# Turning 32x32 blocks by row copies in a hybrid RWKV-7 / HGRN2 layer

## The chip, the cores and the metric

The kernel runs on one core of one Trainium2 chip. The metric is the device time of one execution in microseconds (us). The core's engines are TensorE (PE in the profile, PEld for its weight loads), VectorE (DVE), ScalarE (ACT), GpSimd (POOL) and SyncE (SP); SP issues nearly all DMAs.

## The reference

One layer over x of shape (1, 512, 2048) in float32, with D_RWKV = D_HGRN = 1024, 16 RWKV heads of 64 and 8 HGRN heads of 128:

```python
proj = jnp.einsum('btd,dc->btc', h, w_in[l])              # 2048 -> 4224 + 4096 columns
rw = _token_shift(proj[..., :RWKV_COLS], shift_mu[l])
hg = proj[..., RWKV_COLS:]
o_rwkv, _ = _rwkv7_branch(rw, ...)
o_hgrn = _hgrn2_branch(hg, ...)
y = jnp.einsum('btc,cd->btd', jnp.concatenate([o_rwkv, o_hgrn], -1), w_out[l])
h = _layer_norm(ALPHA * h + y, ln_w[l], ln_b[l])

# RWKV, per frame t and head (S is 64 x 64)
sa = S @ a_t
S = S * w_t + sa b_t^T + v_t k_t^T
o_t = S @ r_t
# then group norm over the head, * gn_w + gn_b, + sum(r k r_k) * v, * silu(z)

# HGRN, per chunk of frames and head (S is 128 x 128), b = cumsum(log f)
att = (q_t exp(b_t - b_s)) . k_s  for s <= t
o = att @ i + (q exp(b)) @ S
S = S * exp(b_last) + (k exp(b_last - b))^T @ i
# then o * rsqrt(mean(o^2)) * g_norm_w * silu(z)
```

## The kernel before

All float32 products of the two projections are made of three matmuls in a split format (high by high, low by high, high by low). `split` (L405) makes the two halves: ScalarE rounds a block of weights to `wh`, VectorE subtracts to `wl`. Weights come in 156 loads of 512 KB (`load`, L420) into two buffers `wr`; each load holds two parts, and each part feeds 12 main matmuls of 128x512 (`three`, L441). `wh` and `wl` have three buffers each. The input projection runs unit by unit of 128 output columns (`proj`, L472) in the order of `_order` (L39): per group of two RWKV pairs k, r, v, the z of two pairs earlier, and q, f, i, g of two HGRN heads. The output projection (`rows`, L488, and the code below it) follows, and a layer norm.

Everything else is written as generators that yield operations: `rwkv_prep` (a pair of heads: decays, keys, scores), `rwkv_invert`, `rwkv_scan` (eight chunks of 64 frames, two pairs at once), `rwkv_finish` (group norm and gate), `hgrn_heads` and `hgrn_out`. The class `Plan` (L63) interleaves them while the program is built: it keeps a clock for each engine with costs, and after each main matmul it lets the queues of generators issue what could start now (`pump`, `step`). A TensorE operation is issued when its inputs have been ready for 0.35 us (`LEAD`); small TensorE work is grouped into visits (`worth`, `HOLD`). The resulting order on each engine is fixed in the program; at run time the engines go through it in order and wait for semaphores. So the place of an instruction rests on what `Plan` holds to be ready, and a wait that lasts longer on the chip holds up everything behind it on that engine.

Frames must stand on the partitions for some operands and channels for others. There are two ways to turn a block. One is TensorE: `tr` (L320) transposes 128x128 with the identity into PSUM. Before, these turned the keys of a head (`hgrn_out`, three tiles, L1056), the end of a head (four tiles, L1090) and the end of an RWKV pair (`rwkv_finish`, four tiles, L912): 8 x 3 + 8 x 4 + 8 x 4 = 88. The other is `turned` (L385): VectorE transposes each 32x32 block in place (`dtr`), and 16 (or 8) DMAs from SBUF to SBUF, one for each source and target band of 32 partitions, put the blocks where they belong. Before, it turned the keys `bk` and the values `zz` of a pair. Its DMAs stand on SP's queue between the weight loads.

Of the kernel before, what the change touches and what calls it, by code (L numbers as in the profile page):

```python
# [11 lines left out]
ALU = mybir.AluOpType  # L12
# [50 lines left out]
class Plan:  # L63
# [7 lines left out]
    HOLD = {"whole": 0.6, "narrow": 1.0}  # L71
    TURNS = {("main", "whole"): 0.015, ("whole", "main"): 0.033, ("main", "narrow"): 0.1,
             ("whole", "narrow"): 0.1, ("narrow", "main"): 0.26, ("narrow", "whole"): 0.2}
    LEAD = -0.35
    SLACK = 0.6
    EARLY = 0.5

    def __init__(self, room):
        self.clock = {"pe": 0.0, "dve": 0.0, "act": 0.0, "pool": 0.0, "dma": 0.0}
        self.table = None  # L80
        self.mode = "main"
# [153 lines left out]
def mixer_kernel(ctx, tc, head, x_r, w_all, par, up, ln_wb, consts, hmask, out):  # L235
# [122 lines left out]
    def dtr(o, i):  # L358
        return dve_op([i], o, lambda: dve.transpose(o, i), per=0.0019)
# [22 lines left out]
            f = lambda: dve.tensor_copy(o, i)  # L382
        return Op([act_way(o, i, AF.Copy, scale), ("dve", 0.075 + size(o) * 0.00105 + moved(o, i), f)], [i], [o])

    def turned(dst, src, tmp, rows=4, base=0):  # L385


        name = dst.tensor.name
        yield dtr(tmp, src)
        yield lambda: by_now(tmp)  # L390
        for a in range(4):
            for b in range(rows):
                o = base + 32 * b
                nc.sync.dma_start(dst[o : o + 32, :, 32 * a : 32 * a + 32],
                                  tmp[32 * a : 32 * a + 32, :, 32 * b : 32 * b + 32])
# [217 lines left out]
            ups.append(upw)  # L613

    hc = [slice(64 * h, 64 * h + 64) for h in range(2)]

    def rwkv_prep(S, p):
        if p == 0:
# [111 lines left out]
        S["bv"] = r  # L730

        yield room(zz=1)
        z = take("zz", [P, NCH, P])
        yield room(ksq=1)
        tmp = take("ksq")
        yield from turned(z, chunks(v), chunks(tmp), rows=2, base=64)
        drop(v, tmp)
        S["zz"] = z

    def from_v(SS, sc):  # L740

        yield lambda: all("zz" in S for S in SS)
        zs = [S["zz"] for S in SS]
        yield room(main=2, mix=1)
        yield landed(*zs, sc)
        pss = [take("main") for _ in SS]
        for half, (z, ps) in enumerate(zip(zs, pss)):
            for c in range(NCH):
                for h in range(2):
                    yield mm(ps[hc[h], c * C : c * C + C], sc[64:128, 0, half * 16 + 2 * c + h],  # L750
                             z[64:128, c, hc[h]])

        def keep():
            for z, ps in zip(zs, pss):
                for h in range(2):
                    yield copy(z[0:64, :, hc[h]], chunks(ps[hc[h]]))
                drop(ps)

        return keep

    def outputs(SS, sc):

        yield room(mix=2)
        pss = [take("mix") for _ in SS]
        for half, (S, po) in enumerate(zip(SS, pss)):
            z = S["zz"]
            yield lambda z=z: by_now(z)
            for c in range(0, NCH, 2):
                for h in range(2):
                    for e in range(2):  # L770
                        yield mm(po[hc[e], c // 2 * P + 64 * h : c // 2 * P + 64 * h + 64],
                                 sc[:, 1, half * 16 + 2 * (c + e) + h], z[:, c + e, hc[h]])
# [52 lines left out]
    def rwkv_scan(SS, sc):  # L825
# [9 lines left out]
        def block(ps, h):  # L835
            return ps[hc[h], h * 64 : h * 64 + 64]

        for rt, bds, o in zip(rts, bdss, os):
            yield memset(rt[64:128], 0.0)
            for t in bds:  # L840
                yield memset(t, 0.0)
            yield memset(o[0:64, 0], 0.0)
        olds = [None] * 2
        for c in range(NCH):
            more = c < NCH - 1
            zs = [zz[:, c] for zz in zzs]
            news = [bds[c % 2] for bds in bdss]
            pxs = []
            if c > 0:
                yield landed(*olds)  # L850
                yield room(mix=2)
                for ar, old in zip(ars, olds):
                    pxs.append(take("mix"))
                    yield mm(pxs[-1][:, :P], ar[:, c], old)
                for rt, px, z in zip(rts, pxs, zs):
                    yield stt(rt[0:64], px[0:64, :P], -1.0, z[0:64], ALU.mult, ALU.subtract)
                if more:
                    for new, old, pc in zip(news, olds, pcs):
                        yield act(new, old, AF.Copy, scale=pc[:, c : c + 1])
            else:  # L860
                for rt, z in zip(rts, zs):
                    yield copy(rt[0:64], z[0:64], scale=-1.0)
            yield landed(*rts)
            yield room(mix=2)
            psas = [take("mix") for _ in SS]
# [2 lines left out]
                yield mm(psa[:, :P], sc[:, 0, i : i + 2].rearrange("p h t -> p (h t)"), rt)  # L868
            for psa, z in zip(psas, zs):
                for h in range(2):  # L870
                    yield copy(z[0:64, hc[h]], block(psa, h))
# [18 lines left out]
    def rwkv_finish(S, p):  # L890
# [14 lines left out]
        drop(sm, sq)  # L905
# [11 lines left out]
        drop(po)  # L917
        yield stt(z, sz, 1.0, z, ALU.add, ALU.mult)
        yield stt(g, g, hcol(HGB, p), z, ALU.add, ALU.mult)
        drop(z, S["bv"], S["ot"], sz)  # L920
        put_gated(p, g)

    def rwkv_group(SS, grp):
        yield lambda: all("scored" in S for S in SS)
        sc = scores[grp]
        yield from rwkv_invert(SS, sc)

        def run():
            yield from rwkv_scan(SS, sc)
            yield from outputs(SS, sc)  # L930
            drop(sc)
            for i, S in enumerate(SS):
                plan.add(finishes, rwkv_finish(S, 2 * grp + i))

        plan.add(scans[0], run())

# [113 lines left out]
    def hgrn_out(S, h, q, k, dt_, dg, tot, tots):  # L1050
# [1 line left out]
        yield room(g=1)  # L1052
        g = take("g")
        kt, state = tiles(g)[:, 0:3], tiles(k)[:, 0:3]
        yield landed(k)
        ps = take("mix")  # L1056
        for t in range(3):
            yield tr(ps[:, t * P : t * P + P], k[:, t * P : t * P + P])
        yield copy(kt, tiles(ps)[:, 0:3])
        drop(ps)  # L1060
        yield has(S, "i")
        yield room(rs=1)
        i_all = S["i"]
# [25 lines left out]
        yield landed(o2)  # L1089
        pn = take("mix")  # L1090
        for j in range(4):
            yield tr(pn[:, j * P : j * P + P], o2[:, j * P : j * P + P])
        yield has(S, "g")
        yield stt(g, pn, hcol(HHW, h), S["g"], ALU.mult, ALU.mult)
        drop(S["g"], pn, o2)
        put_gated(8 + h, g)

    def silu2(ps, put):
# [24 lines left out]


    scans = [plan.queue(), plan.queue()]
    groups, finishes, preps = plan.queue(), plan.queue(), plan.queue()
    heads, stores = plan.queue(), plan.queue()


# [530 lines left out]
```

## Time and profile before

| what | value |
|---|---|
| three runs | 1053.51, 1053.82, 1051.52 us; median 1053.51 |
| the profiled execution | 1053.89 us |
| its span, first to last instruction | 1052.1 us |
| granted TensorE clock, mean | 0.998 |
| instructions | 18837 |
| DMA packets | 87305, of which 56368 under 512 B |

The profile is of one execution. Its page gives busy time of each engine, the chain of work that ended last, and groups of instructions by source line; a line is often a helper's (L317 is any small matmul, L321 any transposition, L330 a ScalarE copy, L340 a VectorE product or sum, L349 a fused VectorE operation). Names of tiles stand without their numbers. A row of the order of time gives the start, the duration, the engine and line, and what is written from what. Matmuls overlap, so the distance from one start to the next is what an instruction holds of TensorE. A row of a group ends with its busy time, the mean duration in ns of one, and the idle time before it. A row of waits gives the engine and line, what it waited for, the sum in us, the count and the longest.

### The profile page before, as it was taken

To read this page: it belongs to the slowest core of one execution; us is meant where nothing else is said; L and a number is where in the kernel's file an instruction comes from. 1 tells how busy PE (TensorE), PEld (TensorE's weight loads), DVE (VectorE), ACT (ScalarE), POOL (GpSimd) and SP (SyncE) were. 2 spreads that over 40 slices of the span, in tenths; PEclk is the share of its full clock that TensorE was granted. 3 is DMA by queue.
4 is the path that set the end of the run, shared out by engine and by line. 5 is a ranking of instruction groups with operands and counts; after the bars stand their busy time and mean duration, and the time that the engine had idled before them with its cause. 6 is when DMAs were issued, how large, how long until landed. Compare 5 with 4: busy or idle time off the path is not lost.

```text
span 1052.1 us, 18837 instructions
## 1 busy us (share of the span) xinstructions
PE 1042.6 (99%) x7342; PEld 867.6 (82%) x7342; DVE 755.1 (72%) x1653; ACT 438.0 (42%) x867; POOL 37.4 (4%) x81
## 2 busy tenths in 40 slices
PE   9999999999999999999999999999999999999997
PEld 8888888888888888888888888888888788888885
DVE  7475898667769987676688856865998677725556
ACT  6445243444352344552533344525235454323321
POOL 0000000000000000000000000000000001000000
PEclk9999999999999999999999999999999999999999
DMA  8134343222343522223534223234352143545613
GB/s 332 51 104 113 98 112 86 85 79 80 84 123 101 122 80 85 73 91 80 137 83 123 88 66 100 69 91 122 96 125 70 58 166 126 186 128 158 203 61 130
DMA packets 87305, 114.79 MB, mean 109 GB/s; under 512 B 56368, under 2 KB 58160, under 8 KB 87088
## 3 DMA queue, kind: packets, MB, share of 16 engines
q1 hardware_dynamic: 87072, 113.39, 36.5%
q8 instruction: 58, 0.95, 0.4%
q14 instruction: 31, 0.25, 0.1%
q10 hardware_dynamic: 144, 0.20, 0.1%
HBM read 99.92 MB, written 7.34 MB: 102 GB/s over the span
## 4 chain that ended last, share of the span: by engine, by line
PE 99%; DVE 1%; issue 0%; DVEq 0%
PE main L446 74%; PE mix L317 11%; PE mix L446 8%; PE main L1185 3%; PE main L317 2%; PE mix L321 1%; PE mix L1135 0%; DVE inv L349 0%; DVE inv L340 0%; DVE stats L1542 0%; DVEq L1656 0%; DVE mv L1350 0%; DVE mv L345 0%; DVE inv L1133 0%; DVE mv L349 0%
## 5 line engine op out<-in xcount | busy, mean ns | idle before, releaser
L446 PE MATMUL main<-xh,wl 128*128 128x512 f32 x864 | 342.4, 396 | 0.0
L446 PE MATMUL main<-xh,wh 128*128 128x512 f32 x864 | 341.6, 395 | 0.0
L446 PE MATMUL main<-xl,wh 128*128 128x512 f32 x864 | 340.9, 395 | 0.0
L330 ACT ACTIVATE wh<-wr 128x512 fp32r<-128x512 f32 x299 | 186.8, 626 | 234.9 <-PE main L446 167.2
L340 DVE TENSOR_TENSOR wl<-wr,wh 128x512 fp32r<-128x512 f32 x299 | 203.7, 682 | 61.2 <-ACT wh L330 59.7
L446 PEld LDWEIGHTS main<-xh,wl 128*128 128x128 f32 x864 | 162.7, 188 | 33.0
L446 PEld LDWEIGHTS main<-xl,wh 128*128 128x128 f32 x864 | 162.7, 188 | 32.8
L446 PEld LDWEIGHTS main<-xh,wh 128*128 128x128 f32 x864 | 162.8, 188 | 32.6
L446 PE MATMUL main<-wh,xh 128*128 128x512 f32 (+1 forms) x262 | 102.4, 391 | 0.0
L446 PE MATMUL main<-wh,xl 128*128 128x512 f32 (+1 forms) x262 | 102.1, 390 | 0.0
L446 PE MATMUL main<-wl,xh 128*128 128x512 f32 (+1 forms) x262 | 102.1, 390 | 0.0
L446 PEld LDWEIGHTS main<-wl,xh 128*128 128x128 f32 x262 | 49.2, 188 | 9.8
L446 PEld LDWEIGHTS main<-wh,xl 128*128 128x128 f32 x262 | 49.2, 188 | 9.7
L446 PEld LDWEIGHTS main<-wh,xh 128*128 128x128 f32 x262 | 49.2, 188 | 9.5
L331 ACT ACTIVATE t<-main,om 128x512 f32<-128x512 f32 x33 | 22.4, 687 | 53.5 <-PE main L446 42.3
L349 DVE SCALAR_TENSOR_TENSOR t<-main,pr,t 128x511 f32<-128x511 f32 x33 | 24.4, 747 | 28.1 <-ACT t L331 27.7
L340 DVE TENSOR_TENSOR inv<-inv,inv 64x30 f32<-64x30 f32 (+14 forms) x120 | 38.6, 322 | 2.9
L340 DVE TENSOR_TENSOR inv<-inv 64x30 f32<-64x30 f32 (+14 forms) x120 | 38.4, 320 | 2.3
L340 DVE TENSOR_TENSOR t<-t,tot 128x256 f32<-128x256 f32 x96 | 37.9, 415 | 1.9 <-PE mix L317 1.7
L349 DVE SCALAR_TENSOR_TENSOR bd<-mix,pc,bd 64x64 f32<-64x64 f32 x112 | 31.7, 283 | 9.5 <-PE mix L317 7.2
L330 ACT ACTIVATE zz<-mix 64x64 f32<-64x64 f32 x61 | 13.4, 219 | 45.6 <-PE mix L317 43.9
L331 ACT ACTIVATE t<-main 128x512 f32<-128x512 f32 x32 | 18.5, 598 | 30.6 <-PE main L446 30.2
(222 smaller groups left out, 1331.2 us busy)
## 6 DMA issues: line engine op xcount, KB each, us to landing
wr<-w_all SPq DMA_DIRECT2D x156, 512.0 KB, 3.6
q<-head SPq DMA_DIRECT2D x15, 448.0 KB, 5.5
q<-q SPq DMA_DIRECT2D x128, 32.0 KB, 2.4
g<-x_r SPq DMA_DIRECT2D x16, 256.0 KB, 4.0
spill<-g SPq DMA_DIRECT2D x12, 256.0 KB, 2.8
out<-q SPq DMA_DIRECT2D x12, 256.0 KB, 2.4
t<-spill SPq DMA_DIRECT2D x10, 256.0 KB, 4.0
zz<-ksq SPq DMA_DIRECT2D x64, 32.0 KB, 2.7
```

The lines of the kernel that those rows point to most:

```text
L317: return Op([("pe", cost, lambda: pe.matmul(o, l, r, start=start, stop=stop, **kw))], [l, r], [o], mode="narrow" if narrow else "main" if ...
L321: return Op([("pe", 0.11, lambda: pe.transpose(o, i, ident))], [i], [o])
L330: return "act", cost, lambda: sc_e.activation(o, i, f, scale=scale)
L331: return "act", cost, lambda: sc_e.activation(o, i, f, scale=scale, bias=bias)
L340: return dve_op([a, b], o, lambda: dve.tensor_tensor(o, a, b, f), base=0.16 if o.shape[0] < P and size(o) == C and o.tensor.name in tags e ...
L349: return dve_op([a, b], o, lambda: dve.scalar_tensor_tensor(o, a, s, b, f1, f2), per=0.00113, base=0.085 if o.shape[0] == P else 0.25 if s ...
L446: pe.matmul(ps, l, r, start=first and i == 0, stop=last and i == 2)
L1185: pe.matmul(pss[a], *ops, start=k == 0 and low == of == 0, stop=k == KT - 1 and low == 1)
```

## The change

1. `turned` moves whole rows. VectorE's transposition now writes its result with the target band outside, so that each of the 16 (8) DMAs has one contiguous piece for each of its 32 partitions (1 KB, 512 B or 384 B) in source and target; before it was 8 pieces of 128 B. The target is therefore laid out by bands, `[band, chunk, 32]`. The values `z` stay in that layout and their readers index it (`hb`, `by32`). For the keys a copy brings it back to `[chunk, 128]`. `Plan` now spaces the four rounds of DMAs by 0.15 us a copy (0.4 before), and holds a block to be ready 2.6 us after the last round's pause (3.0 before).
2. The RWKV ends (8 pairs) are turned in this way and no longer on TensorE. A ScalarE operation reads the turned block, scales it and adds the bias; a sum and a product on VectorE replace two fused operations.
3. For heads 0 to 5 the keys and the end are turned so too; ScalarE or VectorE copies them out of the bands. Heads 6 and 7 stay on TensorE.
4. `REST`: after a narrow TensorE operation no new visit of narrow ones begins for 1.5 us. The finishes of the two pairs of a group have a queue each.

```diff
+    REST = 1.5
...
+            if op.mode == "narrow":
+                self.rest = end + self.REST
...
+        if op.mode == "narrow" != self.mode and now < self.rest:
+            return False
...
-    def turned(dst, src, tmp, rows=4, base=0):
-        name = dst.tensor.name
-        yield dtr(tmp, src)
+    def turned(dst, src, tmp, base=0):
+        n = src.shape[2] // 32
+        yield dtr(tmp, src.rearrange("p c (b f) -> p b c f", f=32))
         yield lambda: by_now(tmp)
         for a in range(4):
-            for b in range(rows):
+            for b in range(n):
                 o = base + 32 * b
-                nc.sync.dma_start(dst[o : o + 32, :, 32 * a : 32 * a + 32],
-                                  tmp[32 * a : 32 * a + 32, :, 32 * b : 32 * b + 32])
-            at = plan.clock["pe"] + 0.4 * rows
+                nc.sync.dma_start(dst[o : o + 32, a], tmp[32 * a : 32 * a + 32, b])
+            at = plan.clock["pe"] + 0.15 * n
             yield lambda: plan.clock["pe"] >= at
-        plan.ready[name] = (plan.clock["pe"] + 3.0, "dma")
+        for t in (dst, tmp):
+            plan.ready[t.tensor.name] = plan.busy[t.tensor.name] = (plan.clock["pe"] + 2.6, "dma")
...
-        yield from turned(bk, bk, tmp)
-        drop(tmp)
+        flat = bk.rearrange("p c t -> p (c t)")
+        yield from turned(blocks(flat, NCH), bk, blocks(tmp.rearrange("p c t -> p (c t)"), NCH))
+        yield copy(tmp.rearrange("p c (a f) -> p a c f", f=32), blocks(flat, NCH))
+        drop(bk)
+        S["bk"] = tmp
...
+        yield from turned(blocks(S["ot"], 4), o_all, blocks(sq.rearrange("p a b -> p (a b)"), 4))
...
-        yield landed(o_all)
-        po = take("mix")
-        for j in range(4):
-            yield tr(po[:, j * P : j * P + P], o_all[:, j])
         yield act(sz, z, AF.Tanh, scale=0.5)
-        yield stt(g, po, hcol(HGW, p), S["bv"], ALU.mult, ALU.add)
+        yield act(in_blocks(g), blocks(S["ot"], 4).rearrange("p a c f -> p c a f"), AF.Identity,
+                  scale=hcol(HGW, p), bias=hcol(HGB, p))
         yield stt(z, sz, 1.0, z, ALU.add, ALU.mult)
-        yield stt(g, g, hcol(HGB, p), z, ALU.add, ALU.mult)
+        yield tt(g, g, S["bv"], ALU.add)
+        yield tt(g, g, z)
...
+        if h < 6:
+            yield from turned(blocks(tmp[:, : 3 * P], 3), tiles(k)[:, 0:3], blocks(g[:, : 3 * P], 3))
+            yield copy(in_blocks(g)[:, 0:3], blocks(tmp[:, : 3 * P], 3).rearrange("p a c f -> p c a f"))
...
+        if h < 6:
+            yield from turned(blocks(o2, 4), tiles(o2), blocks(tmp, 4))
+            yield has(S, "g")
+            yield act(in_blocks(g), blocks(o2, 4).rearrange("p a c f -> p c a f"), AF.Copy, scale=hcol(HHW, h))
+            yield tt(g, g, S["g"])
```

The order of instructions shows it at three places. The first is TensorE in the scan of the first group, at the chunk where `zz` meets the keys `q`; before, seven transpositions (L321) of two heads stood ahead of the scan's two products:

```order
L446 MATMUL main_2152<-xl_91,wh_2130 128x512
L321 MATMUL mix_2199<-cst,t_971 128x128 x4
L321 MATMUL mix_2209<-cst,t_1292 128x128 x3
L317 MATMUL mix_2214<-zz_832,q_447 128x128
L317 MATMUL mix_2215<-zz_1231,q_885 128x128
L446 MATMUL main_2152<-xh_75,wl_2131 128x512
```

After, at the chunk of the same kind (L461 is the main matmul now, L324 the small one):

```order
L461 MATMUL main_2149<-xl_87,wh_2091 128x512
L461 MATMUL main_2149<-xh_71,wl_2092 128x512
L461 MATMUL main_2149<-xh_72,wh_2129 128x512
L461 MATMUL main_2149<-xl_88,wh_2129 128x512
L324 MATMUL mix_2183<-zz_837,q_735 128x128
L324 MATMUL mix_2184<-zz_1233,q_1107 128x128
L324 MATMUL mix_2180<-ia_1840,g_2082 128x128 x3
L461 MATMUL main_2149<-xh_72,wl_2130 128x512
```

The visit holds the scan's products, and with them the head's states from the keys `g`, but no transposition.

The second is SP's queue where the third group's keys are turned. Before, 8 copies at most stand between two weight loads (`wr`):

```order
L423 DMA wr_5044<-w_all 128x1024
L394 DMA q_4116<-q_5022 32x8x32 x8
L423 DMA wr_5082<-w_all 128x1024
L394 DMA q_4116<-q_5022 32x8x32 x8
L423 DMA wr_5141<-w_all 128x1024
```

After, with the ends of two pairs and a head (`t`) turned there as well:

```order
L438 DMA wr_5209<-w_all 128x1024
L402 DMA q_3970<-q_5185 32x256 x12
L402 DMA t_2616<-ksq_5106 32x128 x4
L402 DMA q_3970<-q_5185 32x256 x4
L402 DMA t_2616<-ksq_5106 32x128 x4
L438 DMA wr_5264<-w_all 128x1024
L402 DMA t_2616<-ksq_5106 32x128 x8
L402 DMA t_3391<-ksq_5108 32x128 x16
L438 DMA wr_5344<-w_all 128x1024
L402 DMA t_3641<-ksq_5322 32x128 x12
L438 DMA wr_5384<-w_all 128x1024
```

24 copies stand between two weight loads there, twice in a row.

The third is ScalarE in the same scan as the first place. Before, between weight splits (`wh`) stand the scan's scalings and copies (`bd`, `zz`, `t`):

```order
L330 ACTIVATE wh_2403<-wr_2277 128x512
L330 ACTIVATE wh_2422<-wr_2277 128x512
L330 ACTIVATE bd_2031<-bd_2032,pc_627 128x128
L330 ACTIVATE bd_2033<-bd_2034,pc_1006 128x128
L331 ACTIVATE t_2443<-main_2302,om 128x512
L330 ACTIVATE zz_1231<-mix_2449 64x64 x2
```

After, the reader of the turned end of a head, `g<-t`, stands among them:

```order
L337 ACTIVATE wh_2353<-wr_2205 128x512
L337 ACTIVATE g_2082<-t_972,half 128x512
L337 ACTIVATE wh_2378<-wr_2265 128x512
L337 ACTIVATE bd_2034<-bd_2033,pc_627 128x128
L337 ACTIVATE bd_2036<-bd_2035,pc_1007 128x128
L337 ACTIVATE zz_1233<-mix_2404 64x2x32 x2
```

An instruction that reads what a DMA brings now stands ahead of a weight split and of the scan's scalings.

More of the change, by code (lines that the diff above doesn't have):

```diff
@@ L80, in __init__ @@
         self.table = None
-        self.mode = "main"
+        self.mode, self.rest = "main", 0.0
         self.queues, self.waiting, self.hurry = [], {}, False
@@ L615, in mixer_kernel @@
     hc = [slice(64 * h, 64 * h + 64) for h in range(2)]
+    hb = [slice(2 * h, 2 * h + 2) for h in range(2)]
     def rwkv_prep(S, p):
@@ L732, in rwkv_prep @@
         yield room(zz=1)
-        z = take("zz", [P, NCH, P])
+        z = take("zz", [P, 4, NCH, 32])
         yield room(ksq=1)
         tmp = take("ksq")
-        yield from turned(z, chunks(v), chunks(tmp), rows=2, base=64)
+        yield from turned(z, chunks(v), blocks(tmp, NCH), base=64)
         drop(v, tmp)
@@ L755, in keep @@
                 for h in range(2):
-                    yield copy(z[0:64, :, hc[h]], chunks(ps[hc[h]]))
+                    yield copy(z[0:64, hb[h]], ps[hc[h]].rearrange("p (c a f) -> p a c f", c=NCH, f=32))
                 drop(ps)
@@ L845, in rwkv_scan @@
             more = c < NCH - 1
-            zs = [zz[:, c] for zz in zzs]
+            zs = [zz[:, :, c] for zz in zzs]
             news = [bds[c % 2] for bds in bdss]
@@ L861, in rwkv_scan @@
                 for rt, z in zip(rts, zs):
-                    yield copy(rt[0:64], z[0:64], scale=-1.0)
+                    yield copy(by32(rt[0:64]), z[0:64], scale=-1.0)
             yield landed(*rts)
@@ L870, in rwkv_scan @@
                 for h in range(2):
-                    yield copy(z[0:64, hc[h]], block(psa, h))
+                    yield copy(z[0:64, hb[h]], by32(block(psa, h)))
                 drop(psa)
@@ L1054, in hgrn_out @@
         kt, state = tiles(g)[:, 0:3], tiles(k)[:, 0:3]
[L1055 to L1060, printed above, removed]
+        if h < 6:
+            yield room(ksq=1)
+            tmp = take("ksq")
+            yield from turned(blocks(tmp[:, : 3 * P], 3), tiles(k)[:, 0:3], blocks(g[:, : 3 * P], 3))
+            yield copy(in_blocks(g)[:, 0:3], blocks(tmp[:, : 3 * P], 3).rearrange("p a c f -> p c a f"))
+            drop(tmp)
+        else:
+            yield landed(k)
+            ps = take("mix")
+            for t in range(3):
+                yield tr(ps[:, t * P : t * P + P], k[:, t * P : t * P + P])
+            yield copy(kt, tiles(ps)[:, 0:3])
+            drop(ps)
         yield has(S, "i")
@@ L1088, in hgrn_out @@
         S["used"]()
[L1089 to L1095, printed above, removed]
+        if h < 6:
+            yield room(ksq=1)
+            tmp = take("ksq")
+            yield from turned(blocks(o2, 4), tiles(o2), blocks(tmp, 4))
+            drop(tmp)
+            yield has(S, "g")
+            yield act(in_blocks(g), blocks(o2, 4).rearrange("p a c f -> p c a f"), AF.Copy, scale=hcol(HHW, h))
+            yield tt(g, g, S["g"])
+            drop(S["g"], o2)
+        else:
+            yield landed(o2)
+            pn = take("mix")
+            for j in range(4):
+                yield tr(pn[:, j * P : j * P + P], o2[:, j * P : j * P + P])
+            yield has(S, "g")
+            yield stt(g, pn, hcol(HHW, h), S["g"], ALU.mult, ALU.mult)
+            drop(S["g"], pn, o2)
         put_gated(8 + h, g)
```

20 lines of the change are left out of this document (13 added, 7 removed).

## Prediction

> **What bounds the kernel now.** I read the page's busy line and chain first, then the waits of TensorE, then the order of time around one visit that the change removes, then the queues.
>
> ```profile
> PE 1042.6 (99%) x7342; PEld 867.6 (82%) x7342; DVE 755.1 (72%) x1653; ACT 438.0 (42%) x867; POOL 37.4 (4%) x81
> PE 99%; DVE 1%; issue 0%; DVEq 0%
> PE mix L317 <- issue: 2.0, 1, 2.0
> PE mix L317 <- ACT ksq L1402: 1.5, 1, 1.5
> PE mix L1135 <- DVE inv L1133: 1.1, 1, 1.1
> ```
>
> TensorE is the bound: the chain that ends last lies on it for 99% of the span, and the last three rows are all of its waits, 4.6 us in 1052.1. Busy time of a pipelined engine can flatter, so the starts decide. The rows of TensorE around the turning of an RWKV end (start, duration):
>
> ```profile
> 281.00 0.39 PE L446 MATMUL main<-xl,wh 128*128 128x512 f32 x1
> 281.23 0.39 PE L446 MATMUL main<-xh,wl 128*128 128x512 f32 x1
> 281.46 0.60 PE L321 MATMUL mix<-cst,t 128*128 128x128 f32 x4
> 281.81 0.48 PE L446 MATMUL main<-xh,wh 128*128 128x512 f32 x1
> 282.13 0.40 PE L446 MATMUL main<-xl,wh 128*128 128x512 f32 x1
> 282.36 0.40 PE L446 MATMUL main<-xh,wl 128*128 128x512 f32 x1
> ```
>
> Main matmuls start 0.23 us apart. Four transpositions take 281.46 to 281.81, 0.35 us, and the first main one after them holds 0.32 instead of 0.23: 0.44 us for four, 0.11 each. An instruction taken off this engine is time off the end, as long as no wait appears in its place.
>
> **The change, part by part.** *Transpositions off TensorE.*
>
> ```profile
> L321 PE MATMUL mix<-cst,t 128*128 128x128 f32 x88 | 12.9, 273 | 0.0
> ```
>
> Of these 88 the change leaves 14 (two heads, three plus four each): 8 pairs x 4 and 6 heads x 7 go, 74. At 0.11 that is 8.1 us. The columns' 273 ns each is pipelined length, not price; 74 x 0.273 = 20 us would be too much.
>
> *The pause between narrow visits.* TensorE's order has 30 stretches with narrow matmuls before and 30 after, so I price it at nothing; it changes with whom they share a stretch. A stretch more or less is worth the 0.09 us of the row at 281.81, so some five either way are +-0.5 us.
>
> *VectorE and ScalarE.* The prices:
>
> ```profile
> L359 DVE STREAM_TRANSPOSE ksq<-t 128x512 f32<-128x512 f32 x8 | 5.6, 699 | 0.0
> L349 DVE SCALAR_TENSOR_TENSOR g<-mix,half,t 128x512 f32<-128x512 f32 x16 | 12.0, 747 | 9.0 <-PE mix L321 8.9
> L349 DVE SCALAR_TENSOR_TENSOR g<-g,half,t 128x512 f32<-128x512 f32 x8 | 6.0, 746 | 0.1
> L340 DVE TENSOR_TENSOR t<-t,ksq 128x512 f32<-128x512 f32 x8 | 5.5, 688 | 0.1
> L331 ACT ACTIVATE t<-mix,half 128x512 f32<-128x512 f32 x16 | 10.5, 686 | 16.1 <-PE mix L317 16.1
> 237.00:263.00 26.00, 26.00 (x129) 21.84 (x129) 19.93 (x47) 12.87 (x25) 0.00 (x0) 1.00 0.27 81
> 789.00:815.00 26.00, 26.00 (x355) 21.51 (x354) 21.78 (x44) 13.42 (x31) 0.00 (x0) 1.00 0.23 66
> ```
>
> VectorE gains 14 transpositions of 128x512 at 0.70 and 6 of 128x384 (by length 0.52), 12.9 us; 22 fused operations at 0.75 become 22 products or sums at 0.69, -1.3. ScalarE gains 14 scaled copies at 0.69 and 7 copies of the 1024-wide keys (twice 0.69 at most; an eighth stands on VectorE, +1.4): 19 us. So about +13 and +19 us in a thousand. In the stretches where the RWKV scans run (the last two rows: start and end, length, then TensorE, weight loads, VectorE, ScalarE) VectorE is busy 20 to 22 of 26 us and ScalarE 13, and TensorE all 26; these rows are the cover, and I cost the work at nothing. Without cover it would be the 0.7 us of one operation in a scan's chain.
>
> *Issue on the SP queue.* This is the unknown. 192 small copies become 512, all on the queue that also brings the weights. Rows of that queue (start, duration, then the two lines' minimum/median/maximum in ns):
>
> ```profile
> 0.74 0.86 SPq L1149 DMA_DIRECT2D q<-head  x2
> 81.69 5.16 SPq L394 DMA_DIRECT2D q<-q  x8
> L394 SPq DMA_DIRECT2D q<-q x128: 585/608/1749, 75.7 to 769.3; - x128
> L423 SPq DMA_DIRECT2D wr<-w_all x156: 327/328/1347, 16.8 to 991.4; - x156
> DMA to landing us min/median/max: 1.9/2.5/4.9
> ```
>
> A copy of the old kind (32 partitions, 8 pieces of 128 bytes in each, 256 pieces) is issued every 5.16/8 = 0.645 us. Copies of 128 rows, one piece each, follow at 0.86/2 = 0.43, and at 0.33 where the queue had waited before. The new copies are 32 rows of one piece, which no row shows. Upper bound: 0.47, the 0.43 with a gap, if the price is per instruction. Lower bound: in proportion to pieces, 0.43 x 32/128 = 0.11. The line through 0.645 at 256 and 0.43 at 128 gives 0.27 at 32, that through the two minima of the last rows (585 and 327 ns) gives 0.13. I take 0.20, between these two lines, since both kinds of row say that fewer pieces cost less; 0.11 and 0.47 stay for the range.
>
> [...]
>
> *When the block is wanted.* In the code the first reader of a turned block (a ScalarE copy, except one) is placed 4 x 0.6 + 2.6 = 5.0 us of TensorE work behind the first issue, and the issue itself 0.35 + 0.25 us behind the transposition. Really it can read after fifteen more issues and a landing: 15p + 2.5, against 5.6. At p = 0.20 that is 5.5, on time; at 0.27, 1.0 us late; at 0.47, 4.0 us late. Before, the readers of turned blocks were matmuls some hundred main matmuls behind, over 20 us. What is queued behind a ScalarE copy that waits: the next weight split, and in a scan the copies that TensorE's next visit needs. Their margin:
>
> ```profile
> 243.26 0.46 DVE L382 COPY zz<-mix 64x64 f32<-64x64 f32 x2
> 245.12 0.60 PE L317 MATMUL mix<-zz,q 128*128 128x128 f32 x4
> 248.22 0.29 DVE L349 SCALAR_TENSOR_TENSOR bd<-mix,pc,bd 64x64 f32<-64x64 f32 x1
> 249.66 0.60 PE L317 MATMUL mix<-bd,q 128*128 128x128 f32 x4
> ```
>
> The inputs were ready at 243.72 and 248.51, the visits came at 245.12 and 249.66: 1.4 and 1.15 us, say 1.2. So a block under 1.2 us late costs TensorE nothing. Landings of up to 4.9 instead of 2.5 (a weight load ahead on the same engines) will now and then exceed that: 2.4 - 1.2 = 1.2 us at most; I allow one in the twelve heads' blocks, 1.2 us.
>
> *The weights.*
>
> ```profile
> SPq L423 <- DVE wl L340: 512.7, 101, 14.0
> ```
>
> The queue stands at the weight load, waiting for its buffer, some 5 us at a time. One load feeds 24 main matmuls, 5.4 us. The densest place has 24 copies between two loads: 4.8 us at 0.20, which that wait hides; 11.3 at 0.47, which it doesn't.
>
> *Sum.* The profiled execution took 1053.89 us, 1.8 around its span. 1053.9 - 8.1 + 1.2 = 1047.0. The median of the runs, 1053.51, lies 0.4 lower, inside their scatter; I keep 1047.0.
>
> **The rivals.** *1: the price is per instruction (slower).* p between 0.38 (0.33 and a gap) and 0.47. A block is then 15p + 2.5 - 5.6 = 2.6 to 4.0 us late, ScalarE stands at its reader, and TensorE, whose next visit in the scan waits for a copy behind it, loses 1.4 to 2.8 us at each of the twelve blocks that the heads turn: 17 to 34 us, and some 5 more where 24 copies hold up a weight load. Less 8.1 this gives 1063 (17 alone) to 1085 (34 and 5); I price it at 1068, 17 and 5. It decides from the point where 12 x (lateness - 1.2) eats 8.1: lateness 1.9, p = 0.33. For it: the row at 0.74, with pieces of 1 KB as the new ones have. Against it: 128 to 256 pieces cost half as much again, though the instruction count was the same. Chance 0.28.
>
> *2: the gain is eaten.* p near 0.33, or the wait for the landing long at half the blocks: 8 us saved, 6 to 10 lost, 1051.5 to 1055.5. Chance 0.07.
>
> *3: TensorE had room.* Weight loads are busy 82%, so the transpositions would have lain in idle slots and nothing is saved: 1053.5. [...] Against it: the starts at 281.46 to 282.13, which move by the full 0.44. Chance 0.03.
>
> *4: the end (slower).* The last two pairs' blocks are turned with 32 copies a few us before the output projection reaches them; on the old path only four transpositions stood there. If the queue is held up by loads of the spilled parts, the projection stands for up to 15 x 0.27 + 4.9 - 5.6 = 3.4 us each, and the same at the four pairs before it: 20 us for six, less 8.1, 1066. Chance 0.05.
>
> One more spread: a hole in TensorE that no wait explains, and the lower clock after it (0.94 in the last row):
>
> ```profile
> 816.04 0.45 PE L317 MATMUL mix<-t,t 128*32 128x16 f32 x33
> 818.54 0.44 PE L317 MATMUL mix<-t,t 128*32 128x16 f32 x29 [2.05 <-issue]
> 815.00:842.00 27.00, 24.95 (x365) 21.08 (x364) 18.55 (x66) 11.62 (x34) 0.00 (x0) 0.94 0.21 64
> ```
>
> It can go or double with another order: 2 to 3 us either way.
>
> **How the numbers follow.** The forecast has 0.57: 1047.0, its own range 1043 (hole gone, no lateness) to 1051 (hole doubled, more late landings). Faster by over 0.2% (2.1 us, about what a measurement of this kernel can tell from none) is 0.57; within it rivals 2 and 3, 0.10; slower rivals 1 and 4, 0.33. For 8 in 10 the range starts at 1042 and takes in rivals 2 and 3 and the lower half of the slower ones: 1067.
>
> **What would show it.** Right: 14 transpositions left; copies of 32 rows at 0.1 to 0.27 us; TensorE's waits still under 7 us; ScalarE's copies of turned blocks with little or no wait for a DMA. Wrong: these copies at 0.33 us and more, ScalarE idle before them for a DMA by over 2 us each, and TensorE waiting in the scans. If the copies are cheap and TensorE still waits, the margin of 1.2 us was the failing step.

## The result and the profile after

| | before | after |
|---|---|---|
| median of the runs | 1052.84 us (4 runs, 1051.52 to 1053.82) | 1230.05 us (4 runs, 1226.30 to 1230.42) |
| the profiled execution | 1053.89 us | 1230.42 us |
| its span | 1052.1 us | 1228.6 us |
| granted TensorE clock, mean | 0.998 | 0.936 |
| DMA packets, of which under 512 B | 87305, 56368 | 59660, 15408 |

The ratio is 1.1674 (95% interval 1.1655 to 1.1693): 17% slower, where 1047.0 and at most 1067 had been forecast. The median of e12_ends_late below leaves out one execution of six, which took 1613.24 us at a granted clock of 0.64. Of the page of the changed kernel, the lines that answer to the first ones of the prediction (busy time, clock in 40 slices, chain by engine):

```profile
PE 1093.1 (89%) x7268; PEld 894.9 (73%) x7268; DVE 760.4 (62%) x1660; ACT 455.0 (37%) x902; POOL 37.2 (3%) x81
PEclk9999899889979899889689999898799999899999
PE 75%; SPq 14%; DMA 4%; DVE 3%; issue 3%; ACT 2%; ACTq 0%; DVEq 0%
```

74 instructions have left TensorE (7342 to 7268), and yet it is busy for 1093.1 us instead of 1042.6: 50.5 more, by the lower clock (110.2 of these us lie in stretches at half clock, before 3.4; by estimate half of each is lost, 55.1 and 1.7). It idles for 1228.6 - 1093.1 = 135.5 us, before for 9.5: 126 more. These two make the 176.5 us by which the span grew. VectorE and ScalarE have hardly more to do (5 and 17 us, where the prediction counted 13 and 19). The chain of work now runs over SP's queue for 14% of the span, which it did not touch before.

The longest rows of TensorE's waits, and of the waits of ScalarE and VectorE for a DMA, name the place, and the group of the new copies on SP gives the price (minimum, median and maximum in ns):

```profile
PE main L461 <- ACT wh L337: 30.1, 7, 7.8
PE mix L324 <- DVE ksq L347: 21.7, 5, 7.3
PE mix L324 <- ACT zz L337: 19.7, 5, 5.9
...
ACT q L337 <- DMA q<-q: 69.6, 7, 13.0
ACT g L337 <- DMA ksq<-g: 40.7, 6, 10.2
ACT g L337 <- DMA t<-ksq: 39.8, 6, 8.8
ACT ksq L338 <- DMA t<-ksq: 35.0, 4, 12.4
ACT wh L337 <- DMA wr<-w_all: 22.3, 5, 9.0
...
DVE ksq L347 <- DMA t<-ksq: 24.8, 4, 6.9
...
DVE ksq L366 <- DMA t<-ksq: 15.1, 1, 15.1
```

```profile
L402 SPq DMA_DIRECT2D t<-ksq x224: 507/588/1722, 236.6 to 1075.0; - x112
L402 SPq DMA_DIRECT2D q<-q x128: 507/582/1727, 75.3 to 931.5; - x128
```

TensorE waits for ScalarE and VectorE, and these wait for copies. The first three rows with a DMA are readers of turned blocks: the pairs' keys (`q`), the heads' keys and the heads' ends. The rows with `ksq` on the left are another kind: nobody reads a block there, an instruction wants the tile `ksq`, of which there are two, and the sixteen copies have not all been read out of it. The row `wh` is the split's wait for weights, 22.3 us here and 21.5 before, so the weights are not what is late. Each wait of TensorE can be followed back in the order of time, through what ended it and what stood ahead of that on its engine. Of the 128.5 us in its 31 waits of over 0.5 us behind the first 5 us of the span, 121.2 us in 25 waits end at a copy of a turned block, and none at a weight load: 44.0 at the eight pairs' keys, 21.6 at the six heads' keys, 16.9 at the heads' ends, and 38.7 at the tile `ksq`.

One place in order of time shows how such a wait reaches TensorE. A head's keys are turned on VectorE, SP copies them, ScalarE reads them, and the scan of a pair stands behind (start, duration; the bracket is the idle time before it and what ended it):

```profile
209.53 0.57 DVE L366 STREAM_TRANSPOSE g<-t 128x384 f32<-128x384 f32 x1
...
210.18 10.01 SPq L402 DMA_DIRECT2D ksq<-g  x16
...
218.65 0.39 PE L324 MATMUL mix<-zz,q 128*128 128x128 f32 x2
...
221.61 0.52 ACT L337 ACTIVATE g<-ksq 128x384 f32<-128x384 f32 x1 [5.83 <-DMA ksq<-g]
222.04 0.61 ACT L337 ACTIVATE wh<-wr 128x512 fp32r<-128x512 f32 x1
222.56 0.43 ACT L337 ACTIVATE zz<-mix 64x64 f32<-64x64 f32 x2
...
223.04 0.80 PE L324 MATMUL mix<-zz,q 128*128 128x128 f32 x2 [4.01 <-ACT zz L337]
```

Sixteen copies take 10.01 us, 0.63 each. The reader goes at 221.61, 11.4 us after the first issue, and ScalarE has stood 5.83 us for it. The copies of `zz`, which have nothing to do with the head, come behind it at 222.56, and TensorE has stood 4.01 us for them. Then the clock; three stretches around this place (start and end, length, busy time and count of TensorE, weight loads, VectorE, ScalarE, GpSimd, granted clock, and two columns on DMA):

```profile
207.00:221.00 14.00, 12.03 (x62) 10.02 (x60) 7.08 (x22) 2.95 (x8) 0.00 (x0) 1.00 0.19 52
221.00:228.00 7.00, 4.96 (x16) 4.28 (x17) 3.13 (x8) 3.13 (x9) 0.00 (x0) 0.51 0.25 77
228.00:235.00 7.00, 7.00 (x42) 6.08 (x41) 2.23 (x6) 1.75 (x3) 1.08 (x2) 1.00 0.24 75
```

From 221 to 228 the clock is 0.51, and main matmuls start 0.43 us apart instead of 0.23. The half clock begins at 221.1, inside the wait, and lasts 6.8 us; 4.9 of these lie behind the wait and lose half, 2.4. So this wait of 4.01 us costs about 6.4, by estimate. The trace has 25 stretches at half clock among the work of this execution, 157 us in all, and one before, of 3.4 us; in both a last one begins within 1 us of the end.

### The profile page after: what moved, and what is told of

Same layout as the page of the kernel before. It is cut to its first block, busy times and chain, and to the rows that moved or that the text cites. A ratio compares the mean times of both kernels' runs of the same rounds, so it can differ in the third digit from the quotient of the medians.

```text
span 1228.6 us, 19273 instructions
## 1 busy us (share of the span) xinstructions
PE 1093.1 (89%) x7268; PEld 894.9 (73%) x7268; DVE 760.4 (62%) x1660; ACT 455.0 (37%) x902; POOL 37.2 (3%) x81
## 2 busy tenths in 40 slices
DMA packets 59660, 119.67 MB, mean 97 GB/s; under 512 B 15408, under 2 KB 30512, under 8 KB 59440
## 4 chain that ended last, share of the span: by engine, by line
PE 75%; SPq 14%; DMA 4%; DVE 3%; issue 3%; ACT 2%; ACTq 0%; DVEq 0%
PE main L461 54%; SPq L402 13%; PE mix L324 9%; PE mix L461 7%; PE main L1223 3%; PE main L324 1%; DMA t<-ksq 1%; DMA ksq<-g 1%; DMA q<-q 1%; DMA big<-ln_wb 1%; DVE wl L347 1%; ACT g L337 0%; ACT wh L337 0%; SPq L438 0%; PE mix L1173 0%
## 5 line engine op out<-in xcount | busy, mean ns | idle before, releaser
L461 PE MATMUL main<-xh,wh 128*128 128x512 f32 x864 | 355.5, 411 | 30.1 <-ACT wh L337 30.1
L461 PE MATMUL main<-xh,wl 128*128 128x512 f32 x864 | 356.9, 413 | 9.8 <-DVE wl L347 9.6
L461 PE MATMUL main<-xl,wh 128*128 128x512 f32 x864 | 355.1, 411 | 0.0
L461 PEld LDWEIGHTS main<-xh,wh 128*128 128x128 f32 x864 | 172.1, 199 | 68.7 <-ACT wh L337 33.6
L461 PEld LDWEIGHTS main<-xh,wl 128*128 128x128 f32 x864 | 172.0, 199 | 48.1 <-DVE wl L347 12.6
L461 PEld LDWEIGHTS main<-xl,wh 128*128 128x128 f32 x864 | 172.0, 199 | 35.9
L461 PE MATMUL main<-wh,xh 128*128 128x512 f32 (+1 forms) x262 | 104.1, 397 | 8.7 <-ACT xh L337 8.7
L461 PE MATMUL main<-wh,xl 128*128 128x512 f32 (+1 forms) x262 | 103.5, 395 | 0.7 <-DVE xl L347 0.7
L461 PE MATMUL main<-wl,xh 128*128 128x512 f32 (+1 forms) x262 | 103.7, 396 | 0.0
L461 PEld LDWEIGHTS main<-wh,xh 128*128 128x128 f32 x262 | 50.3, 192 | 19.6 <-ACT xh L337 9.6
L461 PEld LDWEIGHTS main<-wh,xl 128*128 128x128 f32 x262 | 50.1, 191 | 11.2 <-DVE xl L347 1.0
L461 PEld LDWEIGHTS main<-wl,xh 128*128 128x128 f32 x262 | 50.2, 192 | 10.2
L324 PE MATMUL mix<-ksq,ones_r 128*128 128x512 f32 x32 | 16.4, 561 | 44.2 <-DVE ksq L347 21.7
L324 PEld LDWEIGHTS mix<-ksq,ones_r 128*128 128x128 f32 x32 | 7.3, 232 | 50.6 <-DVE ksq L347 25.2
L347 DVE TENSOR_TENSOR inv<-inv 64x30 f32<-64x30 f32 (+14 forms) x120 | 38.5, 320 | 2.3
```

Source lines behind the costliest of these rows:

```text
L324: return Op([("pe", cost, lambda: pe.matmul(o, l, r, start=start, stop=stop, **kw))], [l, r], [o], mode="narrow" if narrow else "main" if ...
L347: return dve_op([a, b], o, lambda: dve.tensor_tensor(o, a, b, f), base=0.16 if o.shape[0] < P and size(o) == C and o.tensor.name in tags e ...
L461: pe.matmul(ps, l, r, start=first and i == 0, stop=last and i == 2)
```

## The experiments

Theory A: an issue costs 0.63 us whatever is in it, a block lands some 6 us behind the place where `Plan` put its reader, the in-order engine stands there, and TensorE and its clock behind it. Rivals: B, 320 more copies on SP hold up the weights; C, the added work on ScalarE and VectorE; D, the pause. Ratios are to the kernel before, with their 95% intervals.

**The price by itself** (e1_price). Twelve copies in a row of each kind, for example:

```diff
+    for i in range(12):
+        nc.sync.dma_start(b0[i][32:64], ca[i][0:32])       # SBUF to SBUF, 32 rows of 1 KB
+    for i in range(12):
+        nc.sync.dma_start(b5[i], x[P:2 * P, 128 * i:128 * i + 256])   # HBM to SBUF, 128 rows
```

> The whole layer is left out; only copies are made, twelve in a row of each kind, and their spacing on the issuing queue is read. Theory A (one price per instruction, whatever is in it): 32 rows of one 1 KB piece from SBUF to SBUF, 128 rows of one piece, 64 rows, 16 rows, and 32 rows of four pieces all follow at 0.5 to 0.65 us on SP. The prediction's line (price by pieces): 16 rows at 0.1 to 0.15, 32 rows at 0.2, 128 rows at 0.43 us. A third reading (SBUF as source costs more than HBM): HBM to SBUF with 128 and with 32 rows both at 0.33 to 0.43, SBUF to SBUF at 0.6. From ScalarE's queue the same copy holds that queue as long, 0.5 us or more, if the price is the instruction's.

The order of time, one row for twelve copies: SBUF to SBUF with 32 rows from SP (L34) and at the same time from ScalarE's and GpSimd's queue (L59, L62); then, on SP alone, with 128, 64 and 16 rows (L37, L40, L43) and 32 rows of four pieces (L46), HBM to SBUF with 128 and 32 rows (L49, L52), and SBUF to HBM with 128 and 32 (L54, L56):

```profile
5.67 7.90 SPq L34 DMA_DIRECT2D b<-a  x12
5.68 7.60 ACTq L59 DMA_DIRECT2D b<-a  x12
5.94 6.01 POOL L62 DMA_DIRECT2D b<-a  x12 [5.50 <-DMA a<-x]
13.61 7.69 SPq L37 DMA_DIRECT2D b<-a  x12
21.35 7.63 SPq L40 DMA_DIRECT2D b<-a  x12
29.02 7.54 SPq L43 DMA_DIRECT2D b<-a  x12
36.60 7.75 SPq L46 DMA_DIRECT2D b<-a  x12
44.40 5.81 SPq L49 DMA_DIRECT2D b<-x  x12
50.25 6.56 SPq L52 DMA_DIRECT2D b<-x  x12
56.85 5.81 SPq L54 DMA_DIRECT2D dr<-a  x12
62.71 5.55 SPq L56 DMA_DIRECT2D dq<-a  x12
```

From SBUF to SBUF an issue costs 0.63 to 0.66 us on SP (a row's time divided by twelve), with 16 rows as with 128, and with four pieces a row as with one. With HBM on one side it is 0.46 to 0.55. In these rows the price goes by instruction and by where the data lie, not by pieces. The prediction had laid a line through a copy inside SBUF and a load from HBM, and read as an effect of pieces what is one of the two memories. ScalarE's and GpSimd's queues, beside SP's, show 0.63 and 0.50.

**The planner told the price** (e2_told).

```diff
-            at = plan.clock["pe"] + 0.15 * n
+            at = plan.clock["pe"] + 0.63 * n
-            plan.ready[...] = plan.busy[...] = (plan.clock["pe"] + 2.6, "dma")
+            plan.ready[...] = plan.busy[...] = (plan.clock["pe"] + 2.2, "dma")
```

> The changed kernel with the planner told the measured price: 0.63 us a copy instead of 0.15, so that readers stand 4 x 2.52 + 2.2 = 12.3 us behind the first copy instead of 5.0. Nothing else differs. Theory A (readers stand ahead of the landing, ScalarE and VectorE stop there, TensorE waits and its clock halves afterwards): 1046 to 1056 us, TensorE's waits under 15 us, clock at 0.99 or more. Theory B (320 more copies on SP hold up the weights): spreading them softens it, but waits on weight splits stay, 1090 us or more. Theory C (13 us of VectorE and 19 of ScalarE work without cover): the same work stays, so 1150 to 1230 us.

1166.62 us, 1.1069 (1.1050 to 1.1088). Theory A's number failed by over 100 us. The trace says why: `Plan` gives every block its own 10 us, but SP has one queue. Where two blocks are turned at once, 32 copies take 20 us (SP, ScalarE, TensorE):

```profile
992.55 20.14 SPq L402 DMA_DIRECT2D t<-ksq  x32
...
1009.49 0.63 ACT L338 ACTIVATE ksq<-t 128x512 f32<-128x512 f32 x1 [20.22 <-DMA t<-ksq]
...
1013.05 0.79 PE L461 MATMUL main<-wh,xh 128*128 128x512 f32 x1 [18.99 <-ACT xh L337]
```

ScalarE stands 20.22 us for the tile `ksq`, and TensorE 18.99 us behind it, in the output projection. This run's time alone leaves theories B and C open, whose numbers it met. Against B, ScalarE's splits wait for weights for 4.6 us in all (22.3 in the change), and no wait of TensorE goes back to a weight load.

**Copies that nobody reads** (e3_load), in the kernel before.

```diff
+        for a in range(4):
+            for b in range(4):
+                nc.sync.dma_start(unread[sent[0]], cst[32 * a:32 * a + 32, :P])
...
```

> The kernel before, with 320 unread copies of 32 rows by 512 B to HBM added on SP at the places where the change turns its blocks (12 heads' turns and 8 RWKV ends, 16 each); nobody reads them, and the transpositions stay on TensorE. Theory A: no reader, no wait: 1053 to 1058 us. Theory B (the queue holds up the weights): 1100 us and more, with TensorE behind waits for weight splits.

1068.27 us, 1.0142 (1.0127 to 1.0157): between the two numbers. Here ScalarE's wait for weights did grow, from 21.5 us to 51.4, 8.2 at the longest. Its row in this run

```profile
ACT wh L330 <- DMA wr<-w_all: 51.4, 15, 8.2
```

and the same row of the kernel before:

```profile
ACT wh L330 <- DMA wr<-w_all: 21.5, 6, 6.0
```

So theory B is a real mechanism, of 15 us here and not 176; 8.2 us of TensorE's waits go back to a weight load. It may be more for copies inside SBUF: these go to HBM, at a lower price (0.50 and 0.57 us each, four at 284.21 and twelve at 288.84). In the change itself, as shown above, no wait of TensorE goes back to a weight load.

**The pause alone** (e4_pause), in the kernel before: only the lines of `REST`.

> The kernel before with the pause of 1.5 us between narrow visits alone. Theory A and B: 1052 to 1055 us, as the kernel before. Theory D (the pause delays the scans): 1065 us or more, with TensorE waiting behind narrow visits that come late.

1050.04 us, 0.9974 (0.9963 to 0.9985): 2.7 us faster. Theory D falls. The hole of 2.05 us that the prediction had noted at 818.54 is gone from the trace, and with it the 3.4 us at half clock behind it. That is not all of the gain: of the executions of the kernel before that were measured beside this run, those at a granted clock of 1.000, without that half clock, took 1051.53 to 1052.43 us.

**Five instructions a block instead of sixteen** (e5_bounce).

```diff
-        for a in range(4):
-            for b in range(n):
...
-                nc.sync.dma_start(dst[o : o + 32, a], tmp[32 * a : 32 * a + 32, b])
...
+        nc.sync.dma_start(way.rearrange("a p b f -> (a p) b f"), tmp.rearrange("p b c f -> p b (c f)"))
+        at = plan.clock["pe"] + 2.6
+        yield lambda: plan.clock["pe"] >= at
+        for b in range(n):
...
+            nc.sync.dma_start(dst[o : o + 32].rearrange("p a c f -> p a (c f)"),
+                              way[:, :, b].rearrange("a p f -> p a f"))
...
```

> The changed kernel, but a block is turned over a scratch in HBM: one write of all 128 rows, and 2.6 us later one read for each target band, 4 reads of 32 rows with 4 pieces each (2 for the values), so 5 instructions on SP instead of 16. VectorE's transposition, the copies on ScalarE and VectorE and the transpositions gone from TensorE are those of the change; readers stand 7.6 us behind the write. Theory A (the sixteen issues at 0.63 us make the block late, readers stand and TensorE behind them): 1044 to 1056 us, TensorE's waits under 15 us. Theory C (the added ScalarE and VectorE work): 1150 us or more.

1076.99 us, 1.0228 (1.0211 to 1.0246). All the added work on ScalarE and VectorE is still there, more bytes move, and 153 of the 177 us are gone. Theory C falls as the main cause. What remains is, in the main, smaller waits of the same kind, the longest of TensorE's 9.4 us at the end of the last pairs; the landings over HBM are longer than I had placed them, 4.6 us in the median for the write and the reads of the keys, and ScalarE stands at all eight keys:

```profile
ACT q L337 <- DMA q<-way: 36.3, 8, 5.9
```

**Without the heads** (e6_pairs): `h < 6` becomes `h < 0` at both places.

> The changed kernel with all eight heads turned on TensorE as before; keys, values and ends of the RWKV pairs stay on row copies (320 instead of 512 on SP). Theory A: the waits behind the heads' blocks go (ScalarE stood 81 us at them), those at the pairs' keys and at the buffer of the turned ends stay: 1110 to 1160 us. If the heads alone were the cause, as the first rival of the prediction had it: 1050 to 1060 us.

1159.57 us, 1.1012 (1.0996 to 1.1029): some 106 us over the kernel before without one head turned by copies. The pairs' keys wait in a queue that is turning the ends of two other pairs (SP, and ScalarE's reader):

```profile
766.90 17.61 SPq L402 DMA_DIRECT2D t<-ksq  x28
784.62 0.53 SPq L438 DMA_DIRECT2D wr<-w_all  x1
785.19 2.41 SPq L402 DMA_DIRECT2D t<-ksq  x4
787.69 10.04 SPq L402 DMA_DIRECT2D q<-q  x16
...
799.09 1.06 ACT L337 ACTIVATE q<-q 128x1024 f32<-128x1024 f32 x1 [18.40 <-DMA q<-q]
```

**Readers 2.4 us later** (e7_later): 5.0 instead of 2.6 in the last line of `turned`.

> The changed kernel with readers placed 7.4 us behind the first issue instead of 5.0 (5.0 for the landing instead of 2.6); copies are issued as in the change. Theory A: some 30 waits of TensorE become up to 2.4 us shorter each, and the clock loses less behind them: 1130 to 1190 us. Theory B (weights late in the queue) and theory C (more work): 1220 to 1235 us, as the change.

1192.50 us, 1.1319 (1.1299 to 1.1339). 37.5 us come back for one number in the planner. At the first pair's keys ScalarE stood 8.84 us at 86.75 in the change, and stands 6.14 here; TensorE 4.79 at 88.37, and 2.32 here. What is placed 2.4 us later waits 2.7 us less on ScalarE and 2.5 less on TensorE. That is theory A's mark, and neither B nor C has it. The first matmul that reads these keys starts at 210.64 in the change, so what ScalarE stands for at 86.75 is not urgent itself; what stands behind it is.

**Another tile for the turned blocks** (e8_buffer): at four turns the turned block goes into a tile `t` instead of a `ksq`.

> The changed kernel, with the turned blocks of the values, the ends and the heads' keys put into a tile t (18 of these) instead of ksq (2 of these), so that nobody who needs the next ksq stands until sixteen copies have been read out of the last one. Copies, prices and readers' places are those of the change. In the change ScalarE and VectorE stood about 82 of some 270 us at a reused ksq. If that wait is a cause of its own: 1150 to 1200 us. If only the readers of the blocks matter: 1215 to 1235 us.

1207.95 us, 1.1470 (1.1454 to 1.1485), between the two ranges: the reused tile is a cause of its own, but taking it out gains only 22 us. Where ScalarE had stood 35.0 us for `ksq`, and 6.9 at the reader of the same block, the turned end of a pair, it now stands as long at that reader:

```profile
ACT g L338 <- DMA t<-t: 36.3, 5, 11.3
```

**Both mended, over HBM** (e9_bounce_t): the tile `t`, and 4.4 and 4.0 us for the two landings.

> The turn over HBM (5 instructions a block) with two edits: the tile t instead of ksq, and the places set by the landings that the run with this turn showed: reads 4.4 us behind the write, readers 4.0 us behind the last read's pause (10.8 us behind the write instead of 7.6). Theory A: the 23.5 us by which that run was slower than the kernel before were waits for landings and for the buffer: 1046 to 1056 us. Theory C, for this rest: the added 13 us of VectorE and 19 of ScalarE work cost something by themselves: 1062 to 1077 us.

1068.89 us, 1.0149 (1.0136 to 1.0163): 13 above theory A's range and inside theory C's for this rest. Two places make most of it. One is the end of the last pairs, which the projection wants at once (ScalarE, TensorE, and the stretch with its clock):

```profile
913.19 0.81 ACT L338 ACTIVATE g<-t,half 128x512 f32<-128x512 f32 x1 [10.78 <-DMA t<-way]
...
916.23 0.80 PE L465 MATMUL main<-wh,xh 128*128 128x512 f32 x1 [9.46 <-ACT xh L337]
```

```profile
905.00:927.00 22.00, 12.54 (x46) 9.81 (x45) 11.13 (x18) 6.15 (x11) 1.32 (x1) 0.77 0.46 132
```

The wait is 9.46 us. The half clock begins at 910.6, inside it, and lasts 10.2 us, of which 4.6 lie behind the wait and lose 2.3: 11.8 together. This is the place of the prediction's fourth rival: several issues and a landing where four transpositions stood. The other is a scan, where VectorE turns a head's end just ahead of the `bd` that TensorE wants (VectorE, TensorE, and the stretch):

```profile
451.73 0.71 DVE L366 STREAM_TRANSPOSE t<-t 128x512 f32<-128x512 f32 x1
...
453.42 1.41 PE L324 MATMUL mix<-bd,q 128*128 128x128 f32 x4 [1.75 <-DVE bd L356]
```

```profile
449.00:464.00 15.00, 11.16 (x37) 8.73 (x36) 9.25 (x24) 8.24 (x20) 1.01 (x1) 0.66 0.22 72
```

TensorE idles 3.8 us there, and the half clock, 10.2 us from 453.2 on, takes some 4.5 from what it does. This is theory C's mechanism on a small scale; no run tests how much of it is the added turn. Over the span TensorE idles 14.2 us more than before and loses 5.1 more to the clock, and its work is 3.6 shorter, of the 8.1 that the transpositions should give: about 15.8 us together, the difference of the spans.

**Only what is not urgent** (e10_ends, e12_ends_late). The kernel before with the pause; the ends of pairs 0 to 5 and heads 0 to 5 go over HBM, keys, values and the last two pairs stay as before.

> A version that takes only what is not urgent off TensorE: the kernel before with the pause, and the ends of RWKV pairs 0 to 5 and heads 0 to 5 turned over HBM (5 instructions, tile t, readers 15.4 us behind the write); keys and values are turned as before. 12 x 4 = 48 transpositions x 0.11 = 5.3 us less than the kernel with the pause alone (1050.0): Theory A 1044 to 1047 us. Theory C: 1055 us or more, since 12 scaled copies on ScalarE and 12 transpositions on VectorE are added.

1051.96 us, 0.9987 (0.9978 to 0.9996): no better than the pause alone. Its trace has a hole in TensorE in the middle of a row of 256 narrow matmuls without a main one between, and 0.72 of the clock around it:

```profile
604.60 0.64 PE L325 MATMUL mix<-t 128*32 128x16 f32 x52
607.26 0.35 PE L325 MATMUL mix<-t 128*32 128x16 f32 x11 [2.02 <-issue]
```

```profile
604.00:616.00 12.00, 9.97 (x260) 7.95 (x249) 5.73 (x21) 5.95 (x16) 0.00 (x0) 0.72 0.09 31
```

2.02 us of hole and up to 12 x 0.28 = 3.4 us of clock (some 0.5 of them inside the hole) are about what was to be gained, 5.3. So I moved one number, which takes the two visits apart:

```diff
-        at = plan.clock["pe"] + 5.0
+        at = plan.clock["pe"] + 6.0
```

> The version with only the ends turned over HBM, with one number changed: reads 6.0 us behind the write instead of 5.0. This moves two visits of narrow matmuls apart that stood together as a row of 256 in that run, with a hole of 2.02 us in TensorE and 6.8 us at half clock behind it. If that hole and its clock are what ate the gain: 1045 to 1048 us, clock 0.999, no hole. If the added work on ScalarE, VectorE and the queue ate it: 1051 to 1053 us, as that run.

1045.86 us, 0.9934 (0.9921 to 0.9947), 0.7% under the kernel before and so faster than both kernels, with the clock at 1.00 in that stretch:

```profile
600.00:625.00 25.00, 25.00 (x345) 21.22 (x344) 16.13 (x48) 13.32 (x32) 0.93 (x1) 1.00 0.23 65
```

**The transpositions by themselves** (e11_gone), in the kernel before with the pause: the loops of `tr` taken out, the unturned tile read instead.

> The kernel before with the pause, and the 74 transpositions left out without anything in their place: the keys and ends of heads 0 to 5 and the ends of the RWKV pairs are read unturned, so this part of the computation is left out. It measures the gain term of the prediction by itself. By the 0.11 us each that the starts gave: 1050.0 - 8.1 = 1042. If TensorE had room for them (the third rival): 1049 to 1051 us.

1046.42 us, 0.9938 (0.9926 to 0.9949), 3.6 us under the pause alone and not 8. TensorE's busy time fell from 1040.6 to 1032.7 us, 7.9, as forecast; the span fell by only 4.1 (1048.2 to 1044.1), because a wait appeared near the end that the kernel with the pause does not have:

```profile
894.07 0.63 PE L326 MATMUL mix<-cst,t 128*128 128x128 f32 x4 [3.01 <-DVE t L345]
```

## Why the prediction was wrong

- **The failing step is the price of an issue**: "I take 0.20, between these two lines, since both kinds of row say that fewer pieces cost less". It is 0.63, above even the upper bound of 0.47. The row of the old copies, 0.645, was the nearest: also from SBUF to SBUF, also on this queue. I explained it away by its pieces, and the bound was drawn from loads from HBM. With 0.63 the prediction's own formula, 15p + landing - 5.6, gives 15 x 0.63 + 1.8 (the landing that the new copies show) - 5.6 = 5.7 us late. ScalarE stood 5.83 us at 221.61; that the two are so near is in part luck, since at other blocks it stood up to 13.0.
- **The first rival was the right mechanism, but far too small**: 22 us of loss at its price, 39 at its end, where some 184 were lost (176.5 and the 8 that the transpositions give). By its formula with p = 0.63, twelve blocks lose 12 x (5.7 - 1.2) = 54 us, 1100 in all. Missing were the other blocks: it counted the heads' alone, whose keys and ends hold TensorE for 38.5 us, while the eight pairs' keys, whose reader is now a ScalarE or VectorE copy close behind, hold it for 44.0, and the run without the heads still took 1160. Missing were the shared queue (two blocks at once, 20 us), the tile `ksq` that is not free until the copies are read out (38.7 us of TensorE's waits, 22 us by its run), and the clock (53 us more lost at half clock).
- **That readers stood over 20 us behind before** was right (the nearest in the trace is 21: the last copy of `zz` is issued at 778.6, and the first matmul that reads them starts at 799.55), and it explains why the old copies, as dear as the new, cost nothing: there was no wait of TensorE behind them.
- **The transpositions' 8.1 us were right** as work (7.9). As time they gave 4.1 of span, with 3.0 more lost in a new wait, the condition that the prediction had named. The third rival, that TensorE had room, does not fit this.
- **The pause at nothing**: 2.7 us gained. The hole named under "one more spread" goes with it, and its half clock, but the pause gives some more than that.
- **VectorE and ScalarE at nothing** holds as far as the runs go: the version with twelve ends turned off TensorE, with their copies and transpositions, has no new wait of TensorE over 1 us. In e9_bounce_t, with all the blocks, there is one of 1.75 us behind VectorE in a scan.
- **The weights**, at nothing in the sum and at some 5 us in the first rival, were 15 by the run with unread copies, but no wait of TensorE in the change goes back to them. The densest place has 32 copies between two weight loads, from 336.44 on for 20.14 us, where 24 had been counted.
- What stays open: how much would come back if one of these alone were mended. TensorE's waits divide as said above, but with the tile changed the wait moved to the next reader, and the half clock belongs to no one cause.

## What to carry to other kernels

Before replacing a large instruction by many small ones on a queue, take the issue price from the nearest row of the same pair of memories (here 0.63 to 0.66 us on SP inside SBUF, 0.46 to 0.55 with HBM on one side), multiply by all blocks that share the queue at once, and compare with the distance to the first reader in program order. Here a wait on an in-order engine was paid by what stood behind it (5.83 us of ScalarE at 221.61 became 4.01 of TensorE), and on TensorE it was paid again in the clock (4.01 us of wait cost 6.4 by estimate; 3.01 us in e11_gone brought no half clock). What wins here is to move only blocks whose readers can be placed far behind, with few instructions each.

## What was not expected of the hardware

- An issue from SBUF to SBUF holds SP's queue for 0.63 to 0.66 us, whether 16, 32, 64 or 128 rows, one piece each or four; with 32 rows ScalarE's queue for 0.63 and GpSimd's for 0.50; with HBM on one side it holds SP's for 0.46 to 0.55.
- A pause of TensorE of some 2 us beside narrow matmuls came with 3.4 to 6.8 us at half clock: 3.4 at 2.05 us in the kernel before and at 2.09 us in the change, 6.8 at 2.02 us in e10_ends (0.72 over the 12 us around it). With a wait of 4.01 us the clock was 0.51 for 7 us. Not every pause did: a wait of 3.01 us among main matmuls (e11_gone, before 894.07) brought none.
- TensorE can stop inside a row of narrow matmuls with no wait that the profile shows: 2.02 us in the middle of 256 in one visit (e10_ends, before 607.26). It did not when the two visits were apart (e12_ends_late, 25.00 of 25.00 us busy from 600 on). The kernel before has such a hole of 2.05 us in one of its rows of 128, the change one of 2.09 us in its row of 256 (before 726.50) and none in its row of 192. What it waits for there was not tested.
